# Loading the sample's q and k into the mLSTM's tile ring, and giving a discarded square its own tile, in a hybrid encoder layer

## The chip, the cores and the metric

The kernel runs on one core of a Trainium2 chip. The metric is the device time of one execution in microseconds (us), lower is better. The time of a kernel is the median of several executions.

## The reference, cut to what matters

One layer is applied to two sequences, a prompt of 1024 tokens and a sample of 256 tokens, both of width 2048 in float32:

```
hn   = rmsnorm(x);  proj = hn @ w_in            # 2048 -> 9232 columns
att  = neighbourhood_attention(q, k, v, bias) * silu(g)      # 8 heads of 128, 8 x 16 window on a 64-wide grid
h    = mlstm(forward) + mlstm(backward)         # 4 heads of 256, from conv+silu of proj, v and gates
mem  = rmsnorm_per_head(h) * sigmoid(o) * silu(z)
y    = rmsnorm(x + concat(att, mem) @ w_out)
```

For each head of the attention, softmax(q k^T scale + bias) v is computed over the window of each token. The sample is a grid of 4 rows, so that all 256 of its keys are scored at once. For each mLSTM head, gated scores q k^T, states k^T v and their products with q are formed, the result is normalised by its mean square, and gated.

## The kernel before, in words

Products in float32 are made of three matmuls of "high" and "low" halves of each operand: the `split` helpers (L164 to L169) write the high half with ScalarE and the low half with VectorE. Layouts put the feature or key axis on the 128 partitions.

The work comes in this order. First the projection for tokens 0 to 767 (`first_tiles`, `pair_a`, to about 1050 us), then that for tokens 768 to 1279: `proj_v`, `proj_pair` and `pair_s`. Both write q, k, v, the convolved q and k of the mLSTM and the gates to DRAM (`qS`, `kS`, `vS`, `cS`, `cD`, `pT`). From the point where the pool `ap` is opened, just before `hf` is first used, the rest of the second projection and the attention and mLSTM stage are written down together: `run` (L1303 on) steps two lists of units, one of the mLSTM and one of the attention, under high priority, and the projections left over fill the gaps between them. Last comes the output product (L1613), whose tiles take the memory of `ap` when the stage is over.

The order of each engine's instructions is not written by hand. The tile framework plans it when the kernel is built, with a simulated timeline (`schedule_with_timeline_sim=True`), by priority and by when tiles come free, and each engine then takes its instructions strictly in that order, waiting where something is not there yet. A tile with a tag takes one of `bufs` slots of that tag and frees it after its last reader. All loads of this stage are issued by SyncE (`DM`), one queue in order.

The units that matter here:

- The attention's list has, for each head, `na_sample(h)` and then `na_prompt(h)`. `na_sample` loads q and k of the 256 sample tokens (L799, two DMAs of 256 KB), then v, makes two blocks of scores `nas_0s`, `nas_1s` (L773, in `na_softmax`), transposes and multiplies by v. `na_prompt` loads q and k of the 1024 prompt tokens (L844, L845, two DMAs of 1 MB), then four blocks follow, each with two score products `nap_0s`, `nap_1s` (L773), a softmax, transposes (L790) and the product with v (L886 to L901). One step starts a new unit and moves the older ones on, so the sample's load, the prompt's load together with the sample's scores, and the prompt's first scores are three steps in a row.
- Both q/k tiles carry the tag `nqk` with one buffer: the sample uses a corner of the prompt's 16 KB-per-partition tile.
- The mLSTM's list has, for each head, a unit for the sample, four state units and four output units. Its k, q and v tiles (`load_s`, L1072, and `load_v`, L1085), the weighted keys and the split states (`c_split`) all take slots of one tag `hf`, 8 slots of 4 x 272 floats per partition. `load_c` (L1066) loads keys for transposes `tb` (L1120).
- Decay weights, products and gate tiles of the mLSTM take slots of the tag `sml`, 6 slots. So does `jk` (L1258), into which ScalarE writes a square of which only the row sum is used (L1259); 40 of them are made.

The stage's projections that fill gaps are `pc` (L662) and `pv` (L740), with weight tiles `wr`, `wr_v` (L633) and their halves `ws`, `wsv`.

Of the kernel before, what the change touches and what calls it, by code (L numbers as in the profile page):

```python
# [8 lines left out]
F32 = mybir.dt.float32  # L9
F32R = mybir.dt.float32r  # L10
# [3 lines left out]
P = 128  # L14
D = 2048
KT = D // P
TS = 256
TP = 1024
# [27 lines left out]
def kernel(  # L46
# [23 lines left out]
    def f(ap):  # L70
        return ap.bitcast(F32)

    def bank(tag, name):
        return ps.tile([P, 512], F32, tag=tag, name=name, bufs=3 if tag == "pr" else 5)
# [683 lines left out]
    def hf(name):  # L758
        return ap.tile([P, 4 * VP], F32R, tag="hf", name=name, bufs=8)
# [2 lines left out]
        return ap.tile([P, 512], dt, tag="mid", name=name, bufs=6)[:, :n]  # L762

    def sml(name, n=256, dt=F32):
        return ap.tile([P, 260], dt, tag="sml", name=name, bufs=6)[:, :n]

    def na_tile(tag, shape, name, bufs, dt=F32):
        return ap.tile(shape, dt, tag=tag, name=name, bufs=bufs)

    def na_softmax(nm, qs, ks, nkeys, h, boff):  # L770
        b = bank("a", f"{nm}s")
        for i, (a_, b_) in enumerate(((0, 0), (0, 1), (1, 0))):
            PE.matmul(b[:, :nkeys], qs(a_), ks(b_), start=i == 0, stop=i == 2)  # L773
        bt = na_tile("nbt", [P, NAK], f"{nm}bt", 2)[:, :nkeys]
        DM.dma_start(bt, rpb_tab[h, :, boff : boff + nkeys])
        st = na_tile("nst", [P, NAK], f"{nm}st", 3)[:, :nkeys]
        sm = na_tile("sm", [P, 4], f"{nm}sm", 4)
        V.tensor_tensor_reduce(  # L778
            st, b[:, :nkeys], bt, -1.0, 3.0e38, ALU.add, ALU.min, sm[:, 0:1],
        )  # L780
        S.activation(st, st, AF.Exp, bias=sm[:, 0:1], scale=-1.0, accum_out=sm[:, 2:3])
        V.reciprocal(sm[:, 3:4], sm[:, 2:3])
        S.mul(st, st, sm[:, 3:4])
        return st

    def na_transpose(nm, st, order, dst):
        b = bank("a", f"{nm}t")
        n = len(order)
        for i, c in enumerate(order):
            PE.transpose(b[:, i * P : (i + 1) * P], st[:, c * P : (c + 1) * P], ident)  # L790
        bv = b[:, : n * P].rearrange("p (k q) -> p k q", q=P)
        S.copy(dst[0], bv)
        V.tensor_tensor(dst[1], bv, f(dst[0]), op=ALU.subtract)

    def na_sample(h):
        nm = f"nas{h}"
        qk = na_tile("nqk", [P, 4, TP], f"{nm}qk", 1, F32R)[:, :, :TS]
        for i, src in enumerate((qS[h], kS[h])):
            DM.dma_start(f(qk[:, 2 * i : 2 * i + 2]), src[:, :, TP:])  # L799
        yield  # L800
        v = na_tile("nv", [P, 4, 2, P], f"{nm}v", NV, F32R)
        DM.dma_start(
            f(v[:, :2].rearrange("p t z d -> p t (z d)")),
            vS[h // 2][TP:, (h % 2) * 256 : (h % 2 + 1) * 256].rearrange("(t p) x -> p t x", p=P),
        )
        st = [
            na_softmax(
                f"{nm}_{t}", lambda a_: qk[:, a_, t * P : (t + 1) * P],
                lambda b_: qk[:, 2 + b_, :], TS, h, BIAS_S + t * TS,
            )  # L810
            for t in range(2)
        ]
        yield
        pt = na_tile("npt", [P, 2, 768], f"{nm}pt", 1, F32R)
        for t in range(2):
            na_transpose(
                f"{nm}_{t}", st[t], (0, 1),
                [
                    pt[:, z, :512].rearrange("p (s q) -> p s q", s=2)[:, :, t * P : (t + 1) * P]
                    for z in range(2)  # L820
                ],
            )
        yield
        b = bank("a", f"{nm}o")
        for c in range(2):
            for i, (a_, b_) in enumerate(((0, 0), (0, 1), (1, 0))):
                PE.matmul(
                    b[:, :TS], v[:, c, a_], pt[:, b_, c * TS : (c + 1) * TS],
                    start=c == 0 and i == 0, stop=c == 1 and i == 2,
                )  # L830
        o = na_tile("nst", [P, NAK], f"{nm}ot", 3)[:, :TS]
        DM.dma_start(o, pT[GT0 + h][:, TP:])
        V.scalar_tensor_tensor(o, b[:, :TS], 0.5, o, op0=ALU.mult, op1=ALU.mult)
        DM.dma_start(mixT[h][:, TP:], o)
        yield
# [220 lines left out]
    def ml_units(sq, h, gates):  # L1056
        T, off = (TS, TP) if sq == "s" else (TP, 0)
        nc_ = T // 256
        nm = f"ml{sq}{h}"
# [95 lines left out]
        def out_unit(J):  # L1155
            n2 = f"{nm}_{J}"
# [14 lines left out]
            for st in range(2):  # L1171
                i = 2 * J + st
                sb = bank("a", f"{n2}s{st}")
                for dt in range(2):
                    mm3(
                        sb[:, :256], lambda a_: kk[:, a_, dt, st * P : (st + 1) * P],
                        lambda b_: qt[:, b_, dt, :], dt == 0, dt == 1,
                    )
                for d in range(2):
                    hc = d * 4 + h  # L1180
                    lo_, hi_ = (0, 256) if st == d else (st * P, (st + 1) * P)
                    n = hi_ - lo_
                    dd = sml(f"{n2}d{st}{d}", n)
                    ds = slice(st * P, (st + 1) * P)
                    S.activation(
                        dd[:, st * P - lo_ : st * P - lo_ + P], dm[:, d, ds], AF.Exp,
                        bias=bd[:, i, hc : hc + 1],
                    )
                    if st == d:
                        os_ = slice((1 - st) * P, (2 - st) * P)  # L1190
                        S.activation(
                            dd[:, os_], al[:, d, os_], AF.Exp, bias=bo[:, i, hc : hc + 1]
                        )
                    V.tensor_tensor(dd, dd, sb[:, lo_:hi_], op=ALU.mult)
                    ph = (mid if st == d else sml)(f"{n2}p{st}{d}", 2 * n, F32R)
                    ph = ph.rearrange("p (h c) -> p h c", h=2)
                    split(ph[:, 0], ph[:, 1], dd)
                    for e in range(lo_ // P, hi_ // P):
                        pp[d, e, st] = ph[:, :, e * P - lo_ : (e + 1) * P - lo_]
# [40 lines left out]
            for e in range(2):  # L1240
                for d in range(2):
                    hc = d * 4 + h
                    c = e * 2 + d
                    V.tensor_scalar(
                        r[:, c : c + 1], acc[d, e][:, 256:257], em[:, 2 * J + e, hc : hc + 1], None,
                        op0=ALU.max,
                    )
                    V.scalar_tensor_tensor(
                        r[:, c : c + 1], acc[d, e][:, 256:257], -1.0, r[:, c : c + 1],
                        op0=ALU.mult, op1=ALU.max,  # L1250
                    )
                    V.reciprocal(r[:, c : c + 1], r[:, c : c + 1])
                S.mul(hs[:, e, :], acc[0, e][:, :256], r[:, e * 2 : e * 2 + 1])
                V.scalar_tensor_tensor(
                    hs[:, e, :], acc[1, e][:, :256], r[:, e * 2 + 1 : e * 2 + 2], hs[:, e, :],
                    op0=ALU.mult, op1=ALU.add,
                )
                jk = sml(f"{n2}jk{e}")  # L1258
                S.activation(jk, hs[:, e, :], AF.Square, accum_out=r[:, 4 + e : 5 + e])  # L1259
            rsqrt_mean(r[:, 6:8], r[:, 4:6], 2, 256.0)  # L1260
            yield
# [30 lines left out]
        for J in range(nc_):  # L1292
            yield out_unit(J)
# [161 lines left out]
    ap = att_ctx.enter_context(tc.tile_pool(name="att", bufs=2))  # L1455
# [7 lines left out]
    def paced(units, n):  # L1463
# [3 lines left out]
        return [at.get(j, iter(())) for j in range(n)]  # L1467

    na = [[u for h in (2 * i, 2 * i + 1) for u in (na_sample(h), *na_prompt(h))] for i in range(ML_H)]
    run(  # L1470
        [
# [308 lines left out]
```

## Time and profile before

| | us |
|---|---|
| median of 3 runs | 2563.29 |
| lowest, highest | 2563.03, 2566.54 |
| the profiled execution | 2565.18 |
| its span, first to last instruction | 2563.3 |

The profile is of one execution. Times in it are microseconds from the first instruction. PE is TensorE's matmuls, PEld its weight loads, DVE VectorE, ACT ScalarE, POOL GpSimd, SP SyncE; "SPq" marks instructions that issue a DMA. L773 is line 773 of the kernel. A group is written "line engine operation output<-inputs shape xcount"; a wait is written "who line <- whom: us in total, times, longest us"; a timeline row is "start us, us, engine line operation", with the idle time before it and its releaser in brackets. A chain row is "start us, us, what". Names of tiles leave out buffer numbers, so `nap3qk` is the q/k tile of prompt head 3, `nas3qk` that of sample head 3, `mlp_1k` the k tile of the prompt's output unit 1 of any mLSTM head, and `mls_0k` that of the sample's unit. The granted clock is TensorE's, 1.00 at full speed. A busy TensorE is not TensorE at full clock: a matmul at half clock is busy for longer.

### The profile page before, as it was taken

What the parts mean: (1) busy time and instruction counts of PE and PEld (TensorE: products, weight loads), DVE (VectorE), ACT (ScalarE), POOL (GpSimd) and SP (SyncE); (2) the same over time, 40 slices, a digit from 0 to 9 for tenths busy, and PEclk for the clock granted to TensorE, in tenths of its full rate; (3) what the DMA queues carried; (4) which work ended last, traced back from release to release, by engine and by line L of the source; (5) the groups of instructions that cost most, each with busy time, mean ns of one, the idle gap of its engine ahead of it and who ended that gap; (6) DMA issues with size and microseconds to landing.
All of it is one profiled execution on the core that took longest, in us unless ns stands there. A gap on an engine that the chain in (4) does not pass through costs nothing.

```text
span 2563.3 us, 44540 instructions
## 1 busy us (share of the span) xinstructions
PE 2534.0 (99%) x15054; PEld 2368.6 (92%) x15054; DVE 1972.6 (77%) x4029; ACT 1345.0 (52%) x3041; POOL 615.3 (24%) x909
## 2 busy tenths in 40 slices
PE   8999999999999999999999999999999999999998
PEld 8999999999999999999999999998988887788886
DVE  8769888888869798898875866765855665879695
ACT  8535545444444444465655666655745543344444
POOL 0535555444544444410001110100100104000001
PEclk9999999999999999999999999999999999999999
DMA  6546464536434342467768878877867849636237
GB/s 215 174 143 200 143 199 130 179 124 200 125 112 126 101 141 89 154 228 223 239 223 299 297 243 272 293 234 261 286 197 251 277 126 377 202 125 218 85 87 254
DMA packets 303483, 503.03 MB, mean 196 GB/s; under 512 B 48752, under 2 KB 191256, under 8 KB 303256
## 3 DMA queue, kind: packets, MB, share of 16 engines
q1 hardware_dynamic: 299096, 484.46, 58.9%
q0 software_dynamic: 4160, 15.73, 1.6%
q8 instruction: 119, 1.95, 0.3%
q14 instruction: 108, 0.88, 0.1%
HBM read 373.13 MB, written 126.95 MB: 195 GB/s over the span
## 4 chain that ended last, share of the span: by engine, by line
PE 92%; DMA 5%; DVE 2%; issue 1%; ACT 1%; SPq 0%; POOL 0%; ACTq 0%; POOLq 0%; DVEq 0%
PE pc L662 16%; PE po L1613 14%; PE pv L740 5%; PE fb L274 2%; PE A24b L274 1%; PE A12b L274 1%; PE A16b L274 1%; PE A44b L274 1%; PE A48b L274 1%; PE A52b L274 1%; PE A40b L274 1%; PE A20b L274 1%; PE A8b L274 1%; PE A50b L274 1%; PE A42b L274 1%; PE A22b L274 1%
## 5 line engine op out<-in xcount | busy, mean ns | idle before, releaser
L1613 PE MATMUL po<-wo,mo 128*128 128x512 f32 x1620 | 376.9, 393 | 3.7 <-ACT wo L165 2.8
L1613 PEld LDWEIGHTS po<-wo,mo 128*128 128x128 f32 x1620 | 303.6, 188 | 76.2 <-ACT wo L165 4.2
L166 DVE TENSOR_TENSOR ws<-wr,ws 128x512 fp32r<-128x512 f32 x152 | 104.3, 696 | 53.2 <-ACT ws L165 52.4
L165 ACT CAST ws<-wr 128x512 fp32r<-128x512 f32 x152 | 92.5, 617 | 70.1 <-PE pc L662 57.5
L165 ACT CAST mo<-mb 128x640 fp32r<-128x640 f32 x72 | 51.8, 726 | 92.5 <-PE po L1613 73.7
L116 POOL TENSOR_SCALAR rs<-rs 128x1 f32<-128x1 f32 x10 | 3.4, 341 | 351.2 <-DVE rs L1593 351.1
L166 DVE TENSOR_TENSOR mo<-mb,mo 128x640 fp32r<-128x640 f32 x72 | 59.1, 827 | 27.1 <-ACT mo L165 27.0
L1562 DVE TENSOR_TENSOR y<-y,po 128x512 f32<-128x512 f32 x90 | 58.5, 687 | 11.3 <-PE po L1613 11.0
L165 ACT CAST mo<-ms 128x640 fp32r<-128x640 f32 x40 | 28.9, 726 | 61.1 <-PE po L1613 32.1
L166 DVE TENSOR_TENSOR wsv<-wr_v,wsv 128x512 fp32r<-128x512 f32 x64 | 44.4, 700 | 14.2 <-ACT wsv L165 13.9
L165 ACT CAST wsv<-wr_v 128x512 fp32r<-128x512 f32 x64 | 39.0, 617 | 26.8 <-PE pv L740 15.5
L1576 ACT ACTIVATE jk<-y 128x512 f32<-128x512 f32 x40 | 25.2, 631 | 36.5 <-DVE y L1562 36.2
L413 DVE SCALAR_TENSOR_TENSOR pcv<-pco,cw_sb,pcv 128x516 f32<-128x516 f32 x48 | 36.7, 764 | 7.1 <-ACT pcv L407 7.0
L166 DVE TENSOR_TENSOR mo<-ms,mo 128x640 fp32r<-128x640 f32 x40 | 32.8, 823 | 7.6 <-ACT mo L165 7.6
L129 ACT ACTIVATE xq<-xq 128x1024 f32<-128x1024 f32 x20 | 21.2, 1061 | 31.7 <-DMA xq<-in_xtok_dram 29.2
L1081 POOL MEMSET mls_0v<- 128x2 f32 x4 | 0.4, 102 | 145.1 <-DVE S_dt.float L166 119.7
L274 PE MATMUL fb<-xg,fw 128*128 128x384 f32 x192 | 34.6, 334 | 0.0
L251 DVE TENSOR_TENSOR pco<-pc,rstdb 128x512 f32<-128x512 f32 x30 | 20.6, 687 | 17.8 <-PE pc L662 17.1
L274 PEld LDWEIGHTS fb<-xg,fw 128*128 128x128 f32 x192 | 33.4, 188 | 0.0
L778 DVE CUSTOM_DVE_ANT_0 nap_0st<-nap_0s,nap_0bt 128x384 f32<-128x384 f32 x32 | 17.7, 555 | 20.1 <-PE nap_0s L773 8.7
L1525 DVE TENSOR_TENSOR ms<-mb,mb 128x640 f32<-128x640 f32 x40 | 32.8, 823 | 0.0
L1492 POOL DMA_DIRECT2D mb<-mx x32 | 17.7, 554 | 58.8 <-DVE ws L166 24.8
(2655 smaller groups left out, 8512.4 us busy)
## 6 DMA issues: line engine op xcount, KB each, us to landing
wr<-in_w_in_dram SPq DMA_DIRECT2D x76, 512.0 KB, 4.7
wr_v<-in_w_in_dram SPq DMA_DIRECT2D x32, 512.0 KB, 5.0
wb<-in_w_o_dram SPq DMA_DIRECT2D x48, 256.0 KB, 3.0
xq<-in_xtok_dram SPq DMA_DIRECT2D x20, 512.0 KB, 4.2
mb<-mx POOLq DMA_DIRECT2D x32, 320.0 KB, 8.2
wr_wp<-in_w_o_dram SPq DMA_DIRECT2D x16, 512.0 KB, 4.0
vS<-vo SPq DMA_DIRECT2D x24, 256.0 KB, 5.1
nap_0bt<-in_rpb_tab_dram SPq DMA_DIRECT2D x32, 192.0 KB, 4.3
```

Of the source, the lines that this page charges most:

```text
L129: S.activation(raw, raw, AF.Square, accum_out=ssq[g][:, t, q : q + 1])
L165: S.copy(hi, src)
L166: V.tensor_tensor(lo, src, f(hi), op=ALU.subtract)
L251: V.tensor_tensor(o, src, rb, op=ALU.mult)
L274: PE.matmul(o, w(a_), x(b_), start=first and m == 0, stop=last and m == 2)
L413: V.scalar_tensor_tensor(dst[:, a:n], src[:, a + j - pad : n + j - pad], cw_sb[:, ct, j : j + 1], dst[:, a:n], op0=ALU.mult, op1=ALU.add,)
L662: PE.matmul(pb[j], t[j][:, wi, c : c + P], xs[xi], start=first and m == 0, stop=last and m == 2,)
L740: PE.matmul(outs[tt], xs[:, tt * P : (tt + 1) * P], t[:, wi, q * w : (q + 1) * w], start=first and m == 0 and (gates or tt % 2 == 0), stop ...
L1525: V.tensor_tensor(t, x, y_, op=op)
L1562: V.tensor_tensor(Y[p, q, tt], Y[p, q, tt], bk, op=op)
L1576: S.activation(jk, Y[p, q, tt], AF.Square, accum_out=ss[t][:, c : c + 1])
L1613: PE.matmul(bk[tt], m[xi][:, tt * P : (tt + 1) * P], w[wi], start=first and kk == 0 and j == 0, stop=last and j == 2, skip_group_check=True,)
```

## The change

The q and k of a sample head go into a tile of the `hf` ring (4 x 256 of its 4 x 272 floats) and no longer into the tile that the prompt uses. The discarded square has a tag and a tile of its own with one buffer, and the `sml` tag has 7 slots. Nothing that is computed changes, and no instruction is added or removed.

```diff
     def sml(name, n=256, dt=F32):
-        return ap.tile([P, 260], dt, tag="sml", name=name, bufs=6)[:, :n]
+        return ap.tile([P, 260], dt, tag="sml", name=name, bufs=7)[:, :n]
...
     def na_sample(h):
         nm = f"nas{h}"
-        qk = na_tile("nqk", [P, 4, TP], f"{nm}qk", 1, F32R)[:, :, :TS]
+        qk = hf(f"{nm}qk")[:, : 4 * TS].rearrange("p (i c) -> p i c", i=4)
         for i, src in enumerate((qS[h], kS[h])):
             DM.dma_start(f(qk[:, 2 * i : 2 * i + 2]), src[:, :, TP:])
...
-                jk = sml(f"{n2}jk{e}")
+                jk = ap.tile([P, 256], F32, tag="jk", name=f"{n2}jk{e}", bufs=1)
                 S.activation(jk, hs[:, e, :], AF.Square, accum_out=r[:, 4 + e : 5 + e])
```

## The prediction

> **What bounds the kernel now.** I read the page first, then TensorE's waits, then the stretch of the trace in which the edited lines run.
>
> ```profile
> span 2563.3 us, 44540 instructions
> PE 2534.0 (99%) x15054; PEld 2368.6 (92%) x15054; DVE 1972.6 (77%) x4029; ACT 1345.0 (52%) x3041; POOL 615.3 (24%) x909
> PE 92%; DMA 5%; DVE 2%; issue 1%; ACT 1%; SPq 0%; POOL 0%; ACTq 0%; POOLq 0%; DVEq 0%
> ```
>
> TensorE is busy for 2534.0 of 2563.3 us and carries 92% of the chain that ended last. The change neither adds nor removes a matmul, so directly it can win only idle time of TensorE and time in which TensorE's clock is low. The edited lines run in the attention and mLSTM stage, about 1350 to 2110 us. Its row in the table by windows (TensorE busy first, then weight loads, VectorE, ScalarE, GpSimd, then clock, DMA share, GB/s), and TensorE's waits in the same stretch:
>
> ```profile
> 1350.00:2110.00 760.00, 754.89 (x4813) 684.68 (x4812) 512.76 (x1396) 448.57 (x1114) 68.59 (x252) 1.00 0.78 255
> ```
> ```profile
> PE nap_0s L773 <- DMA nap3qk<-kS: 2.5, 1, 2.5
> PE nap_0s L773 <- DMA nap4qk<-kS: 1.9, 1, 1.9
> PE nap_0s L773 <- DMA nap2qk<-kS: 0.5, 1, 0.5
> ```
>
> TensorE idles 760 - 754.89 = 5.11 us here, and three waits make up 2.5 + 1.9 + 0.5 = 4.9 us of it: the first prompt scores of heads 3, 4 and 2 wait for the prompt's k. All else in the stage, ScalarE at 448.57 and VectorE at 512.76 of 760 us among it, lies beside a full TensorE.
>
> Why that k is late can be read at head 3, from SyncE's queue, TensorE's timeline and the chain (start, duration, what):
>
> ```profile
> 1594.95 0.68 PE L773 MATMUL nap_1s<-nap2qk 128*128 128x384 f32 x3
> ...
> 1595.66 0.53 SPq L799 DMA_DIRECT2D nas3qk<-qS  x1
> ```
> ```profile
> 1619.46 0.51 PE L773 MATMUL nas_1s<-nas3qk 128*128 128x256 f32 x3
> ```
> ```profile
> 1623.45 0.52 SPq L844 DMA_DIRECT2D nap3qk<-qS  x1
> 1624.02 0.60 SPq L845 DMA_DIRECT2D nap3qk<-kS  x1
> ```
> ```profile
> 1624.02 10.22 DMA nap3qk<-kS
> 1634.25 0.14 issue
> 1634.38 0.76 PE nap_0s L773 x3
> ```
>
> One buffer serves in turn: prompt 2's last scores (1594.95), then sample 3's load (1595.66), then sample 3's last scores (1619.46), and only then the prompt's two loads of 1 MB (1623.45, 1624.02). The second takes 10.22 us, and TensorE, in its written order, stands before it for 2.54 us.
>
> **What a stall costs beside itself.** TensorE's clock in windows of 2 us, at the 0.5 us stall of head 2, after that of head 3 and after that of head 4 (the clock is the third number from the end):
>
> ```profile
> 1554.00:1556.00 2.00, 1.50 (x10) 1.47 (x10) 0.38 (x2) 0.00 (x0) 0.00 (x0) 1.00 1.10 343
> 1634.00:1636.00 2.00, 1.62 (x10) 1.61 (x11) 0.82 (x3) 0.00 (x0) 0.00 (x0) 0.92 1.08 361
> 1636.00:1638.00 2.00, 2.00 (x11) 2.00 (x11) 1.83 (x6) 1.93 (x6) 1.04 (x3) 0.50 1.10 386
> 1638.00:1640.00 2.00, 2.00 (x15) 2.00 (x15) 1.35 (x5) 0.20 (x2) 0.73 (x4) 0.73 1.01 405
> 1734.00:1736.00 2.00, 2.00 (x9) 2.00 (x10) 0.97 (x3) 0.00 (x0) 0.60 (x1) 0.66 1.02 412
> 1736.00:1738.00 2.00, 2.00 (x11) 2.00 (x10) 1.55 (x7) 1.17 (x4) 0.00 (x0) 0.50 1.02 348
> 1738.00:1740.00 2.00, 2.00 (x18) 2.00 (x18) 0.81 (x3) 1.68 (x6) 0.00 (x0) 0.98 0.87 230
> ```
>
> After the 2.5 us stall the clock falls short by (0.08 + 0.50 + 0.27) x 2 us = 1.7 us of full speed; after the 1.9 us stall by (0.34 + 0.50 + 0.02) x 2 = 1.7 us. After 0.5 us nothing. TensorE counts as busy meanwhile, so this 3.4 us stands in no idle column.
>
> [...]
>
> **The change part by part.**
>
> Prompt's buffer. With the sample elsewhere, the loads of L844 and L845 wait only for the previous prompt's last scores: at head 3 they could be issued at about 1595.7 instead of 1623.45, 27.7 us sooner. Landing in 10.2 us, as in this row, they are there by about 1606, before the sample's scores at 1619.46 and 28 us ahead of their own. Heads 2 and 4 are built alike. If TensorE's first prompt scores keep their place behind the sample's, all three stalls go: -4.9 us, and with the two long ones -3.4 us of low clock. Bounds: nothing (the planner pulls the scores up to the earlier landing) and -8.3 us. I take -8.3: the sample's scores, too, stand 24 us behind the issue of their load, which needs 5 (below), so the stream is held there by something other than loads, and the prompt's first scores come after it.
>
> Sample's load. The same two DMAs of 256 KB go into one of eight "hf" tiles; no instruction is added. Their time to landing, from the tile of sample 1:
>
> ```profile
> DMA to landing us min/median/max: 4.5/4.7/5.0
> ```
>
> The new wait is on SyncE, for a free slot; behind it stand bias tiles, weights and the mLSTM's own loads. Such waits exist already:
>
> ```profile
> SPq L1085 <- PE mlp_0s L1095: 10.7, 3, 5.0
> ...
> SPq L799 <- PE pc L662: 7.7, 2, 7.2
> ```
>
> The new one is bounded by the longest ring wait, 5.0 us; the old one on L799, up to 7.2 us, goes. What the borrowed slot delays is a prefetch, and those have room:
>
> ```profile
> 1428.01 0.52 SPq L1072 DMA_DIRECT2D mlp_1k<-cS  x1
> ```
> ```profile
> 1461.37 0.52 PE L1095 MATMUL mlp_1s<-mlp_1q,mlp_1k 128*128 128x256 f32 x3
> ```
> ```profile
> 1516.43 1.33 SPq L1085 DMA_DIRECT2D mlp1a2v<-vS  x1
> ```
> ```profile
> 1564.00 0.77 PE L1095 MATMUL mlp1a2kv<-mlp1a2v,mlp1a2w 128*128 128x258 f32 x5
> ```
>
> One is used 33 us after issue, the other 48; a slot held from load to scores (24 us at head 3) fits. I take 0. Without that room each late tile of 512 KB would cost up to the 5.0 us of a ring wait.
>
> The jk tile and seven "sml" slots. Nothing but ScalarE writes jk, nothing reads it:
>
> ```profile
> L1259 ACT ACTIVATE mlp_2jk<-mlp_2hs x8: 417/418/420, 1516.1 to 2074.6; 128x256 f32<-128x256 f32 x8
> ```
>
> Forty squares stay forty at 0.42 us on an engine with 311 us free in the stage. Two requests fewer per mLSTM unit and one slot more can only loosen that chain; TensorE idles 5.11 - 4.9 = 0.2 us for everything else there, so the gain is 0 to 0.2 us. I take 0. A loss could come only through the rearranged order of the stage, which is the third rival.
>
> End of the stage. It has room too:
>
> ```profile
> 2113.31 0.34 PE L901 MATMUL nap_3o<-nap_3pt,nap_3v 128*128 128x128 f32 x2
> ```
> ```profile
> 2185.08 12.99 PE L1613 MATMUL po<-wo,mo 128*128 128x512 f32 x55 [0.47 <-DVE wo L166]
> 2199.01 1.65 PE L1613 MATMUL po<-wo,mo 128*128 128x512 f32 x6 [0.94 <-ACT wo L165]
> ```
>
> The last attention matmul is at 2113.31, and gate projections fill some 70 us until the output product at about 2183. An earlier or later end of attention by 10 us is absorbed. The small idles here, 0.47 + 0.94 = 1.4 us, may come or go.
>
> **Sum.** The profiled execution took 2565.18 us: 2565.2 - 4.9 - 3.4 = **2556.9**, I say 2557. That execution is 1.9 us above the median, 2563.29 us (2563.03 to 2566.54), so against the median it is -6.3 us, -0.25%. About 0.2%, 5.1 us, is what a measurement of this kernel can tell from no change: faster is below 2558.2, slower above 2568.4.
>
> **Rivals.**
>
> 1. The sample's load becomes the late one, because a slot comes free late. It lands in 4.5 to 5.0 us, half the prompt's time; half of 4.9 us in pieces too short for a dip is 2.5 us: 2556.9 + 2.5 = 2559.4, the same. For it: SyncE's ring waits. Against: its room of 24 - 5 = 19 us at head 3. 0.13.
>
> 2. It does not do what it says: the first scores are pulled up to the landing, the stalls only move in time, 2563 to 2565, the same. For it: TensorE's place at head 3 (1634.38 - 2.54 = 1631.8) is 7.8 us behind the load's issue, about a load's time, so the planner may set it by the load. 0.07.
>
> 3. Slower: the moved 2 MB crowd out loads that have no room. At the start of the stage (the window's clock, DMA share and GB/s last; then the chain):
>
> ```profile
> 1370.00:1380.00 10.00, 9.88 (x78) 9.42 (x77) 4.33 (x16) 5.11 (x12) 0.13 (x2) 1.00 1.04 404
> ```
> ```profile
> 1363.74 7.47 DMA mlp0a3cv<-cD
> 1371.22 0.04 issue
> 1371.26 0.33 PE mlp0a3tb L1120
> ```
> ```profile
> 1370.94 0.52 SPq L844 DMA_DIRECT2D nap0qk<-qS  x1
> ```
>
> The DMA engines are full, the tile for the transposes at 1371.26 lands as it is needed, and prompt 0's loads, now behind it, need no longer wait for the sample's scores. Put ahead of it they delay it by 2 MB / 404 GB/s = 5.2 us, and with a dip of 1.7 us TensorE loses 6.9 us. One such place takes back most of the gain (2563.8); from two on it decides (2570.7); three give 2556.9 + 20.7 = 2577.6. Eight head changes offer the chance. For it: the whole order of the stage is replanned, and TensorE takes its queue in order, whatever is late. Against: room of 33 and 48 us above. 0.30.
>
> 4. The dips come from something other than the stalls and stay: only 4.9 us go, 2565.2 - 4.9 = 2560.3, the same. That both stand right behind the two long stalls speaks against it. 0.05. [...]
>
> My forecast keeps 0.45; its own range is 2553 (the 1.4 and 0.2 us of small idles go too, and the 1.9 us by which the profiled execution is above the median) to 2560.5 (the stall of 1.9 with its dip of 1.7 stays), and 0.40 of it lies below 2558.2. So faster 0.40; same 0.05 + 0.13 + 0.07 + 0.05 = 0.30; slower 0.30. For 8 in 10 the range goes from 2553 to 2578, past three crowded loads, leaving some 0.05 below and 0.12 above.
>
> **What would show it.** Right: no wait of the first prompt scores on their q and k, the prompt's loads issued within a few us of the previous prompt's last scores, TensorE idle under 1 us between 1350 and 2110, no window there with a clock near 0.5. Wrong: waits of TensorE on the sample's tile (rival 1), on the same tile still (2), on mLSTM, v or weight tiles behind a prompt's load (3). A long idle at the output product's start would show that the end of attention had no room after all.

## The result and the profile after

The changed kernel takes 2573.20 us (median of 6 runs, 2572.02 to 2575.65), the kernel before, run beside it, 2562.86 us (6 runs, 2559.49 to 2566.54). The ratio is 1.0043, with a 95% interval of 1.0032 to 1.0055: 10.3 us slower. In a second comparison (e5 below) it is 1.0048 (1.0036 to 1.0060).

The page of the changed kernel, profiled in an execution of 2575.65 us (span, then engines):

```profile
span 2573.9 us, 44495 instructions
...
PE 2536.9 (99%) x15054; PEld 2367.3 (92%) x15054; DVE 1968.2 (76%) x4029; ACT 1338.6 (52%) x3041; POOL 611.5 (24%) x909
```

TensorE is busy for 2.9 us longer than before (2536.9 against 2534.0 us). The shares of the chain that ended last can't be set against those of before: TensorE's reads 75% here, 88% in a second profile of the changed kernel and 37% in a second one of the kernel before, and what is missing up to 100% is the first part of the span, over which the chain was not followed. The table by windows, for the stage and for the 90 us behind it, in which the last gate projections end and the output product begins (TensorE busy first; clock third from the end), of after and then of before:

```profile
1350.00:2110.00 760.00, 752.75 (x4834) 681.77 (x4834) 507.40 (x1399) 445.48 (x1116) 66.54 (x252) 1.00 0.80 255
2110.00:2200.00 90.00, 83.47 (x347) 66.47 (x346) 46.26 (x70) 25.08 (x42) 28.73 (x52) 0.96 0.93 341
```
```profile
2110.00:2200.00 90.00, 86.63 (x374) 69.23 (x374) 52.50 (x79) 27.23 (x44) 28.65 (x52) 1.00 0.90 337
```

Idle time in the stage went up, from 5.11 to 7.25 us, and behind it from 3.37 to 6.53 us, with a clock of 0.96. TensorE's waits show that they are other waits:

```profile
PE po L1613 <- ACT wo L165: 3.8, 1, 3.8
PE mlp_0tp L1266 <- DVE mlp_0hs L1264: 2.0, 1, 2.0
PE pc L662 <- ACT ws L165: 2.0, 2, 1.4
PE pc L662 <- DVE ws L166: 1.6, 2, 1.3
...
```

No wait of the first prompt scores (nap_0s) on their q and k is left. At head 3 it can be seen why; SyncE's queue, then TensorE, of the changed kernel:

```profile
1601.69 0.53 SPq L844 DMA_DIRECT2D nap3qk<-qS  x1
1602.28 0.60 SPq L845 DMA_DIRECT2D nap3qk<-kS  x1
1604.25 0.53 SPq L799 DMA_DIRECT2D nas3qk<-qS  x1
```
```profile
1600.98 0.68 PE L773 MATMUL nap_1s<-nap2qk 128*128 128x384 f32 x3
...
1623.98 0.52 PE L773 MATMUL nas_0s<-nas3qk 128*128 128x256 f32 x3
...
1635.52 0.69 PE L773 MATMUL nap_0s<-nap3qk 128*128 128x384 f32 x3
```

The prompt's loads go out 0.03 us after the previous prompt's last scores end (1601.66), 22 us sooner than before, and now ahead of the sample's. They are used 33 us later. So the change does what it says, and pays elsewhere. Two such places, in rows of the changed kernel: in the middle of the stage (SyncE, ScalarE, TensorE), where a load of 2 KB comes late for ScalarE's first convolution tap, and TensorE's queue, in its written order, stands behind what ScalarE and VectorE have yet to do; and at the output product's start. The chain rows put below those of the first stall show why the small load is late.

```profile
1471.38 0.42 SPq L671 DMA_DIRECT2D pco<-qb  x1
```
```profile
1476.56 0.82 ACT L407 ACTIVATE pcv<-pco,cb_sb,cw_sb 128x516 f32<-128x516 f32 x1 [2.85 <-DMA pco<-qb]
```
```profile
1478.49 0.44 PE L1266 MATMUL mlp_0tp<-ident,mlp_0hs 128*128 128x128 f32 x2 [1.96 <-DVE mlp_0hs L1264]
```
```profile
1464.12 6.82 DMA mx<-nap0o
...
1471.00 0.33 SPq L847
...
1471.38 5.08 DMA pco<-qb
```
```profile
2109.42 0.33 PE L901 MATMUL nap_3o<-nap_3pt,nap_3v 128*128 128x128 f32 x2
...
2178.69 11.57 PE L1613 MATMUL po<-wo,mo 128*128 128x512 f32 x38 [3.82 <-ACT wo L165]
```
```profile
2178.00:2180.00 2.00, 1.31 (x3) 1.12 (x4) 1.33 (x3) 1.98 (x4) 0.00 (x0) 0.50 1.04 396
2180.00:2182.00 2.00, 2.00 (x6) 1.52 (x6) 1.17 (x2) 0.20 (x1) 0.00 (x0) 0.50 1.04 391
2182.00:2184.00 2.00, 2.00 (x7) 1.52 (x6) 0.00 (x0) 0.00 (x0) 0.00 (x0) 0.50 1.06 401
```

At 1478 us SyncE stands until the store of prompt 0's output has freed the tile for the gate of prompt 1 (L847), and the 2 KB behind it go out 5.2 us ahead of their use. Prompt 1's q and k are not what they stand behind: these were issued some 44 us earlier and landed within 10.1 us. At the end, the last attention matmul comes 3.9 us earlier than in the first profile of before (2109.42 against 2113.31), and yet the output product waits 3.82 us for its weights, with three windows at 0.50 behind the wait.

**One account for all kernels.** For each profile I added up, over windows of 2 us from 1350 to 2260 us, TensorE's idle time and the part of its busy time that a clock under 1.00 lost. It is this sum by parts, in us (the names of the experiments are explained below):

| kernel | 1350 to 1400 | to 1700 | to 2100 | to 2260 | sum | span |
|---|---|---|---|---|---|---|
| before, first profile | 0.1 | 4.8 | 3.6 | 3.8 | 12.3 | 2563.3 |
| before, second, third | 0.0, 0.0 | 3.2, 5.1 | 0.0, 0.2 | 3.6, 3.6 | 6.8, 8.9 | 2558.3, 2560.8 |
| changed, first profile | 1.6 | 5.0 | 0.8 | 9.3 | 16.7 | 2573.9 |
| changed, second (e5) | 1.9 | 5.3 | 0.8 | 8.4 | 16.4 | 2570.4 |
| e1 sample's tile alone | 1.6 | 6.9 | 4.0 | 4.9 | 17.5 | 2568.6 |
| e2 square and slot alone | 0.0 | 1.8 | 0.1 | 2.0 | 4.0 | 2555.7 |
| e4 own tile | 1.8 | 2.4 | 1.2 | 8.3 | 13.7 | 2566.0 |
| e3 k stays | 0.5 | 0.5 | 0.0 | 2.1 | 3.1 | 2554.4 |
| e6 head 0 held | 0.0 | 3.0 | 3.5 | 9.4 | 15.9 | 2567.4 |
| e7 columns ahead | 1.6 | 0.0 | 0.0 | 8.9 | 10.5 | 2568.5 |
| e8 burst written later | 3.7 | 5.9 | 0.6 | 9.9 | 20.1 | 2573.0 |
| e9 burst held | 1.7 | 5.2 | 0.9 | 5.1 | 12.9 | 2568.6 |
| e10 all three | 0.0 | 2.4 | 2.6 | 1.9 | 6.9 | 2560.1 |
| e12 slot alone | 0.0 | 0.8 | 0.2 | 2.6 | 3.5 | 2556.1 |
| e15 before, burst held | 0.0 | 4.3 | 0.0 | 0.8 | 5.1 | 2557.0 |
| e16 e2, burst held | 0.1 | 1.0 | 0.9 | 0.8 | 2.7 | 2557.6 |
| e17 columns by GpSimd | 2.2 | 1.2 | 0.7 | 9.8 | 13.9 | 2567.2 |
| e18 small loads by GpSimd | 7.2 | 0.2 | 0.2 | 4.1 | 11.7 | 2568.6 |
| e11 fastest | 0.0 | 0.0 | 0.0 | 0.9 | 0.9 | 2549.7 |

Span less sum is 2549 to 2555 us in all but four rows (changed first, e7, e9, e18), whose profiled executions came to the stage some 4 to 6 us late, with TensorE's instructions ahead of the stage the same. So the kernels differ mainly by idle and low clock in this stretch. The changed kernel's 16.5 against a mean of 9.3 in the three profiles of before are 7 of the 10 us: 5.2 of them at the end, 1.7 at the start, and 0.8 up to 1700 us, where one set of stalls takes the place of another, less 0.5 up to 2100 us. 1 more is idle time in the output product from 2200 to 2500 us (1.4 and 1.8 us against 0.4, 0.0 and 0.7), and the last 2 I did not place.

### The profile page after: what moved, and what is told of

The parts are those of the page before. It is cut to its first block, busy times and chain, and to the rows that moved or that the text cites. A ratio compares the mean times of both kernels' runs of the same rounds, so it can differ in the third digit from the quotient of the medians.

```text
span 2573.9 us, 44495 instructions
## 1 busy us (share of the span) xinstructions
PE 2536.9 (99%) x15054; PEld 2367.3 (92%) x15054; DVE 1968.2 (76%) x4029; ACT 1338.6 (52%) x3041; POOL 611.5 (24%) x909
## 3 DMA queue, kind: packets, MB, share of 16 engines
q8 instruction: 119, 1.95, 0.3%
## 4 chain that ended last, share of the span: by engine, by line
PE 75%; DMA 5%; DVE 5%; issue 1%; ACT 1%; SPq 0%; POOL 0%; ACTq 0%; POOLq 0%; DVEq 0%
PE pc L662 15%; PE po L1613 10%; PE pv L740 4%; PE A16b L274 1%; PE A44b L274 1%; PE A40b L274 1%; PE A48b L274 1%; PE A52b L274 1%; PE A20b L274 1%; PE A54b L274 1%; PE A46b L274 1%; PE A22b L274 1%; PE A18b L274 1%; PE A70b L274 1%; PE A38b L274 1%; PE A50b L274 1%
## 5 line engine op out<-in xcount | busy, mean ns | idle before, releaser
L165 ACT CAST wsv<-wr_v 128x512 fp32r<-128x512 f32 x64 | 39.0, 617 | 26.9 <-PE pv L740 12.9
L274 PE MATMUL fb<-xb,fw 128*128 128x384 f32 x96 | 23.9, 356 | 7.8 <-ACT fw L172 7.8
```

The costliest lines, as they stand in the source:

```text
L165: S.copy(hi, src)
L274: PE.matmul(o, w(a_), x(b_), start=first and m == 0, stop=last and m == 2)
```

## The experiments

Theories: **A**, the prompt's 2 MB, issued earlier (22 us at head 3), come in the way of loads that are asked for just ahead of their use; **B**, the borrowed slot makes the sample's load or the ring late; **C**, the part with the square; **D**, any edit makes the planner write another order with other late places; later **E**, for the end.

**e1, the sample's tile alone; e2, the square's tile and the seventh slot alone.**

```diff
# e1: before, and
+        qk = hf(f"{nm}qk")[:, : 4 * TS].rearrange("p (i c) -> p i c", i=4)
# e2: the changed kernel, but
+        qk = na_tile("nqk", [P, 4, TP], f"{nm}qk", 1, F32R)[:, :, :TS]
```

> Only the sample's q and k move to the hf ring; the square stays in a sml tile and sml keeps 6 slots. Four theories of the loss of 10.3 us. A (moved prompt loads: the 2 MB that now start 12 to 28 us earlier make small and just-in-time loads late, those of the 4 boundary columns qb above all): near the changed kernel, 2573 us, with the same stalls behind the convolution's first tap. B (borrowed slot: the sample's load waits for a free hf slot and is late): near 2573 too. C (the square's tile and the seventh sml slot rearranged the stage): the forecast's 2557. D (every edit makes the planner write a new order with late places of its own, whichever edit it is): another time anywhere from 2557 to 2578, with stalls at other places.

> Only the square gets a tile of its own and sml a seventh slot; sample and prompt share one q/k buffer as before. A and B: 2563, with the three waits of the first prompt scores as before. C: 2573. D: another time between 2557 and 2578, although the sml ring was no bottleneck.

e1: 2568.95 us against 2560.18, ratio 1.003 (1.002 to 1.004), with waits behind ScalarE and the gate rows (`zr`) in the middle of the stage, so at other places than in the changed kernel. e2: 2557.53, ratio 0.9989 (0.9980 to 0.9998), and no wait of the first prompt scores is left although the buffer is still shared: there the prompt's k lands in at most 9.5 us (10.2 us at head 3 before), and TensorE's order has the scores 10 us behind its issue. C falls; the sample's move carries the loss. The waits went because the order moved, which is D at work.

**e3, the sample's k in the shared buffer, its q in the ring; e4, both in a tile of their own.**

```diff
# e3, in place of the two loads (the scores then read k from kk)
+        kk = na_tile("nqk", [P, 4, TP], f"{nm}k", 1, F32R)[:, 2:4, :TS]
+        DM.dma_start(f(qk[:, 0:2]), qS[h][:, :, TP:])
+        DM.dma_start(f(kk), kS[h][:, :, TP:])
# e4
+        qk = na_tile("nsq", [P, 4, TS], f"{nm}qk", 1, F32R)
-        return ap.tile([P, 4 * VP], F32R, tag="hf", name=name, bufs=8)
+        return ap.tile([P, 4 * VP], F32R, tag="hf", name=name, bufs=7)
```

> The changed kernel, but the sample's k stays in the buffer shared with the prompt and only its q takes an hf slot: the prompt's loads are held back until the sample's scores, as before, while the ring still lends a slot. A: back to 2563 (the crowding goes, the stalls of 8.3 us return). B: 2573 or more. D: neither follows; stalls at other places than in both kernels.

> The changed kernel with the sample's q and k in a tile of their own (4 KB per partition), and the hf ring cut from 8 slots to 7 to make room. The prompt's loads are free to go early as in the changed kernel, the sample's load waits for no ring slot. A: 2573 or more. B as a late sample's load: 2563 or less, with the sample's loads back at their earlier places; B as a shortage of ring slots: above 2573, since the ring has 7 all the time. D: another time.

e3, which lends the slot but holds the prompt's loads: 2555.64, ratio 0.9983 (0.9974 to 0.9992), better than A had said, since nearly no stall came back. e4, which lends nothing but lets the prompt's loads go: 2567.39, ratio 1.003 (1.0018 to 1.0041), with the same long idle at the output product and, in addition, waits of 1.3 and 1.1 us for the sample's q. B as the main cause falls; freeing the prompt's loads is what the slow kernels have in common: the changed kernel, e1 and e4 are 3.0 to 4.8 parts in 1000 slower than before, while e2, e3 and e12 (below), which hold them, are 0.4 to 1.7 parts faster (e12 no more than no change can be). Each has an order of its own, so D alone would hardly part them like this, though it settles where each of them loses.

**e5, the changed kernel again.**

> The changed kernel once more, for a second profile. Its first profile is 4.2 us longer than that of before already at the end of the second projection (1351.64 against 1347.46 us), where TensorE's instructions are the same; if that belongs to the one execution, it is gone here (1347 to 1348, as in the four runs so far) and the time is 2569 to 2573; if it belongs to the kernel, 1351 again. The start of the transposes stays 27 to 27.5 us behind the end of the second projection by theory A (23.8 before).

2573.96, ratio 1.0048. The end of the second projection is at 1348.21: the 4.2 us ahead of the stage were that one execution's. The rest came back as in the first profile (16.4 against 16.7 us).

**e6, head 0 held.**

```diff
+        if h:
+            qk = hf(f"{nm}qk")[:, : 4 * TS].rearrange("p (i c) -> p i c", i=4)
+        else:
+            qk = na_tile("nqk", [P, 4, TP], f"{nm}qk", 1, F32R)[:, :, :TS]
```

> The changed kernel, but sample 0 alone keeps its q and k in the buffer shared with the prompt, so that prompt 0's loads are held as before; the other seven heads are free. Theory A: the start of the transposes is back at 23.5 to 24.3 us behind the end of the second projection, 3.3 us sooner than in the changed kernel, and the time falls by about 3.3 us if the rest of the stage stays. Theory B (borrowed slots): no gain at the start. Theory D: the rest of the stage is replanned too, so that the total can go either way by 5 us while the start obeys A.

2566.48, ratio 1.0022 (1.0013 to 1.0030), 7.5 us less than the changed kernel beside it (the profiled execution, 2569.14 us, gained less). The transposes start 23.7 us behind the end of the second projection (27.0 in e5), and the idle there is gone, 1.9 to 0.0 us. VectorE's first bias table shows the crowd, in e6 and then in the first profile of the changed kernel:

```profile
1366.95 0.42 DVE L778 CUSTOM_DVE_ANT_0 nas_0st<-nas_0s,nas_0bt 128x256 f32<-128x256 f32 x1 [1.06 <-DMA nas_0bt<-in_rpb_tab_dram]
```
```profile
1376.20 0.42 DVE L778 CUSTOM_DVE_ANT_0 nas_0st<-nas_0s,nas_0bt 128x256 f32<-128x256 f32 x1 [5.51 <-DMA nas_0bt<-in_rpb_tab_dram]
```

TensorE does not stand before the late tile itself: its order has the transposes later, behind all the `pv` matmuls, and what is then bare is the time of the splits between transposes and their product. The idle near 1458 us went too, with a new order; the end stayed.

**e7, the boundary columns loaded ahead.**

```diff
...
+    for ct in range(16):
+        if QK0 + ct // 2 * 2 not in SECOND:
+            DM.dma_start(qbt[:, ct], qb[ct])
...
-                DM.dma_start(o[:, 0:4], qb[ct])
+                G.tensor_copy(o[:, 0:4], qbt[:, ct])
```

> The changed kernel, but the 4 boundary columns of each convolution of the late projections are loaded ahead of the stage into one small tile, and GpSimd copies them in place of a load of 2 KB by SyncE at each use. By theory A with its detail (the small loads queue behind the 1 MB ones, ScalarE waits 2.7 to 3.4 us for them at its first tap, and TensorE's queue after it), the stalls at 1461, 1478 and 1650 us (1.4 + 2.0 + 1.4 us) go: 4.8 us less. If the small loads are bystanders, ScalarE's waits go but the stalls of TensorE stay.

2570.25, ratio 1.0035 (1.0023 to 1.0047), 3.7 us less. TensorE's busy time from 1400 to 1700 us, in e7 and in e5:

```profile
1400.00:1700.00 300.00, 299.96 (x2023) 277.04 (x2022) 219.29 (x604) 191.86 (x482) 33.84 (x115) 1.00 0.84 273
```
```profile
1400.00:1700.00 300.00, 296.18 (x1996) 273.60 (x1996) 216.84 (x605) 188.25 (x475) 30.04 (x103) 0.99 0.84 270
```

The stalls behind the small loads are gone, all of them. The gain in time is less certain, since the two intervals overlap.

**e8 and e9, the burst at the end.**

```diff
# e8: the 16 tiles of Ac and Aa are written down inside the product
+        if p == 0 and i == 2:
+            Ac.append(mix_block(1, 1, kk))
+        if p == 0 and i == 5:
+            Aa.append(mix_block(0, 0, kk))
# e9: at the same places, behind the step's split, with a tie to its operand
+        V.tensor_copy(t[:, 0:1], f(after[:, 0:1]))
+        G.dma_start(t, mixT[8 * kh + kk][:, th * TH : (th + 1) * TH])
```

> The changed kernel, but of the 10.5 MB that GpSimd loads for the output product in one burst from about 2115 us on, the half that the second and third product need first is asked for only when these products are written down. Theory E (the end of attention came 4 us sooner, the burst with it, and it starves the weight loads of the late gates and of the output product): the wait of 3.8 us at 2179 us, the two of 1.3 to 1.4 us before it and the clock dip behind it go, 6 to 9 us less. If the burst is a bystander: no change in TensorE's waits from 2110 to 2190 us.

> The changed kernel with the burst really held: each of the 16 loads of the second half (5.2 MB) goes into a tile of which VectorE first writes one column, out of the split operand of the second product's first or second step, so that GpSimd cannot load it before. Sixteen copies of one column are added. Theory E (the burst that follows the end of attention starves the last gate weights and the output product's first weights): TensorE's waits on these weights between 2110 and 2190 us (2.2 + 1.3 + 4.4 us in the second profile of the changed kernel) and the clock dip fall to the 1 to 3 us of the kernel before, 6 to 9 us less, 2565 to 2568. If the burst is a bystander (the gate projections are simply further behind): no change, or slower, since the held loads can be late for the second product.

e8: 2574.67, ratio 1.0048. It tells nothing: 31 of these loads are still issued between 2110 and 2190 us, since the planner moved them up as soon as their memory was free. e9: 2566.60, ratio 1.0021 (1.0012 to 1.0031), 6.6 and 7.4 us below the changed kernel's two medians (5.6 and 6.9 us by the ratios, 3 to 4 us in the account above). TensorE's waits from 2110 us on, in the changed kernel and in e9:

```profile
PE po L1613 <- ACT wo L165: 3.8, 1, 3.8
PE pc L662 <- ACT ws L165: 1.4, 1, 1.4
PE pc L662 <- DVE ws L166: 1.3, 1, 1.3
```
```profile
PE pc L662 <- DVE ws L166: 1.9, 1, 1.9
PE pc L662 <- ACT ws L165: 1.5, 1, 1.5
```

The wait at the output product goes, the two in the gate projections stay, beside the first half of the burst, which is not held. But that the burst starved the product is not shown by it. What the product waits for is one weight load (`wr_wp`, 512 KB). Its issue by SyncE and the product's first matmuls, in the kernel before, the changed kernel and e9, then its landing in the changed kernel:

```profile
2153.86 1.47 SPq L633 DMA_DIRECT2D wr_wp<-in_w_o_dram  x1
```
```profile
2160.00 7.10 PE L1613 MATMUL po<-wo,mo 128*128 128x512 f32 x30
```
```profile
2163.31 1.11 SPq L633 DMA_DIRECT2D wr_wp<-in_w_o_dram  x1
```
```profile
2167.75 7.12 PE L1613 MATMUL po<-wo,mo 128*128 128x512 f32 x30
```
```profile
2160.33 0.33 SPq L633 DMA_DIRECT2D wr_wp<-in_w_o_dram  x1
```
```profile
2169.86 15.46 PE L1619 MATMUL po<-wo,mo 128*128 128x512 f32 x66
```
```profile
2163.31 14.63 DMA wr_wp<-in_w_o_dram
```

It takes 14.6 us to land in the changed kernel and still 13.4 us in e9 (the median of the 16 loads of its kind is 4.8 us in the changed kernel). But it is issued 4.4 us ahead of the product's first matmul in the changed kernel, 6.1 us in the kernel before, and 9.5 us in e9, whose order is another. Over all profiles the wait goes with that lead: 3.8 to 5.2 us of wait where the lead is 3.4 to 4.4 us (changed twice, e4, e6, e7, e8, e17), 1.3 to 1.8 us where it is 6.1 to 6.6 us (before three times, e2, e3, e18), and none in the product's first 20 us where it is 8.6 us or more (e1, e9 to e12, e16). An earlier burst, as E has it, does not go with it: its first load is at 2113.17 and 2114.95 us in the two later profiles of the kernel before (e13, e14), and at 2115.13 and 2111.73 us in those of the changed kernel. So by these rows the load's place in SyncE's order makes most of this wait. That is read from the profiles; no run changed the place alone.

**e10, all three at once; e11, e3 with the burst held; e12, the seventh slot alone.**

> The changed kernel with all three suspects taken away at once: head 0's sample back in the shared buffer, the boundary columns loaded ahead, the burst held. Seven heads keep their early prompt loads. If the loss of 10 to 12 us is these three places (3.3 at the start, 3 to 5 at the small loads, 4 to 6 at the end), the stage takes 805 to 808 us from the end of the second projection to the output product (816 in the changed kernel, 812.5 before), and the time is 2557 to 2561, less some us that the 8 small loads cost ahead of the stage. If early loads cost something everywhere else too: 2565 or more.

> The fastest kernel so far (the sample's k in the shared buffer, its q in the ring, own tile for the square, seven slots) with the burst held. By theory E, 0 to 3 us less than 2555.6, since its waits at the output product's start are only 2.6 us. If holding delays the second product: slower.

> The kernel before with nothing but the seventh sml slot; the square stays in the ring. It splits the gain of the square's part (2.6 us by medians, and the three waits on the prompt's k gone although the buffer is still shared). If the extra slot is the cause: 2557 to 2558. If the square's own tile is: 2560 to 2561 with the three waits. By theory D (the planner's order moves with any edit): neither, 2555 to 2570.

e10: 2561.05, ratio 0.9998 (0.9990 to 1.0007): with the three places gone nearly all of the loss is gone, and seven heads of early loads remain. Set against the kernel before with the burst held (e15 below, 0.9989), a loss of 2 us may be left; the intervals overlap. The early loads bring nothing: 2.4 and 2.6 us of new idle stand behind other small loads (`mlp_0zr`, `nas5ot`), and the way from the end of the second projection to the output product takes 812.2 us, not the 805 to 808 expected. e11: 2552.89, ratio 0.9966 (0.9953 to 0.9978), the fastest of all. Its window of the stage:

```profile
1350.00:2110.00 760.00, 760.00 (x4856) 688.65 (x4855) 517.55 (x1404) 451.20 (x1119) 73.40 (x260) 1.00 0.79 258
```

TensorE is never idle in the stage. e12: 2559.91, ratio 0.9996 (0.9987 to 1.0005): the extra slot cannot be told from no change, nor from e2. The waits for the prompt's k are gone here too, with one slot more and nothing else, which is D again.

**e13 and e14, before again.**

> The kernel before once more, for a second profile. Its first profile (2565.18 us) lies at the top of the runs of before (medians 2560.2 to 2562.9), and the forecast took its three waits for the prompt's k (4.9 us) and two clock dips (3.4 us) for every execution's. If they belong to the kernel: the same three waits and dips, 812 to 813 us from the end of the second projection to the output product. If they belong to that execution (a load that lands 2 us later than others): less of them, 804 to 809 us, and about 2557 to 2562 in all.

> The kernel before a third time, for the spread of the same waits. As for the second: the waits for the prompt's k of heads 2, 3 and 4 either again 4.9 us with both dips, or another number.

2560.17 and 2562.65 us. The waits for the prompt's k, in e13 and in e14:

```profile
PE nap_0s L773 <- DMA nap3qk<-kS: 1.6, 1, 1.6
...
PE nap_0s L773 <- DMA nap2qk<-kS: 0.5, 1, 0.5
```
```profile
PE nap_0s L773 <- DMA nap3qk<-kS: 1.8, 1, 1.8
...
PE nap_0s L773 <- DMA nap2qk<-kS: 0.6, 1, 0.6
```

2.1 and 2.4 us, not 4.9; head 4's 1.9 us does not come back, and one dip is left in e14, none in e13. From the end of the second projection to the output product it is 807.5 and 809.5 us, so the first profile's 812.5 were that execution's.

**e15, before with the burst held; e16, e2 with the burst held.**

> The kernel before with the burst held as in the two runs that held it, nothing else changed. It tells whether the end's gain needs the change at all. By theory E, 2 to 4 us less than before (the changed kernel gained 7.4, the fastest one 2.8): 2557.5 to 2559.5. If the gain came from undoing what the change did: 0.

> Own tile for the square and seven slots, both q and k of the sample in the shared buffer, and the burst held. It tells whether moving the sample's q alone is worth anything beside the other two: by the difference of the two kernels without the hold (2557.5 against 2555.6), 2554 to 2556 here against 2552.9; if the q's move is worth nothing, 2553.

e15: 2558.73, ratio 0.9989 (0.9980 to 0.9998); e16: 2558.25, ratio 0.9982 (0.9974 to 0.9991). Holding the burst gains by itself: in e15 the weight load has a lead of 6.6 us, close to the 6.1 us of before, and yet no wait at the product's start is left, and the stretch from 2100 us on costs 0.8 us instead of 3.6 to 3.8. So the burst does count, by some 3 us, in the kernel before as well. e16 is above the 2554 to 2556 us expected. Moving the sample's q alone, e11 over e16, is worth 1.6 parts in 1000, but the intervals touch, so that stays open.

**e17, the boundary columns issued by GpSimd; e18, all small loads.**

```diff
# e17
+                G.dma_start(o[:, 0:4], qb[ct])
# e18: also
+        G.dma_start(bt, rpb_tab[h, :, boff : boff + nkeys])
+                    G.dma_start(o_, pT[OT0 + ch][:, c0 : c0 + na])
+                    G.dma_start(zn, pT[ZT0 + ch][:, c0 : c0 + na])
+        G.dma_start(o, pT[GT0 + h][:, TP:])
```

> The changed kernel, but the loads of 2 KB of boundary columns (12 of them) are issued by GpSimd instead of SyncE, at the same point of the program. Are they late because of their place in SyncE's one queue, or because the DMA engines are full? Place in the queue: ScalarE's waits for them at 1457, 1473 and 1642 us and the stalls of TensorE behind them go, as in the kernel that loads them ahead (2570.3), 2569 to 2571. Full engines: they land as late as before, 2573 to 2574. A new order of the stage can cover either by some us, so the waits for these loads decide, not the time alone.

> As the one before, and also the bias tables (128 to 192 KB), the mLSTM's gate rows and the sample's gate (up to 128 KB) are issued by GpSimd, so that SyncE's queue holds the large loads, the weights and the stores. If the loss of the changed kernel is small loads behind large ones in one queue: the idle at the stage's start (1.6 to 1.9 us) and between 1400 and 1700 us (3.8 to 5 us) goes, about 5 us less, 2567 to 2569, while the end (8.4 to 9.3 us of idle and low clock) stays. If GpSimd, which waits up to 46 us for mLSTM tiles, holds them up instead: slower than 2574.

e17: 2568.69, ratio 1.0021 (1.0013 to 1.0030). ScalarE's waits at the first tap in the stage and, of the line that loads the columns, the time to landing: e5, then e17.

```profile
ACT pcv L407 <- DMA pco<-qb: 18.0, 5, 5.3
```
```profile
DMA to landing us min/median/max: 2.8/5.0/6.4
```
```profile
ACT pcv L407 <- DVE wsv L166: 1.5, 1, 1.5
```
```profile
DMA to landing us min/median/max: 1.9/5.1/6.4
```

They take as long to land, but nobody waits for them any more: they are asked for further ahead. Of the 12 loads 8 are used less than 6 us after their issue in the changed kernel's first profile, 6 in e5 and 5 in the kernel before, 2 in e17. (ScalarE waits 9.6 us for them in the first profile of the changed kernel, 5.7 us in the kernel before.) So their place in SyncE's order made them late, with a landing of 5 us in either case. One such load does stand behind a prompt's k, as A has it. In e5 SyncE, before it issues the load that ScalarE then waits 5.28 us for at 1437.65 us, stands until prompt 1's k has landed:

```profile
SPq L671 <- DMA nap1qk<-kS: 3.5, 1, 3.5
```

But TensorE is not idle there. Where it is, at 1461, 1478 and 1650 us in the first profile, the last prompt's loads had been issued 33 us or more before. Issued by another engine these loads land no faster, 5.1 us in e17 against 5.0 us in e5 (the medians); what helped is the time at which they are issued.

e18: 2566.85, ratio 1.0015 (1.0006 to 1.0024). From 1400 to 2100 us 0.4 us is left, and the end is at 4.1 us, half of what was expected to stay. At the start the third rival's place shows (SyncE, then TensorE):

```profile
1363.31 0.52 SPq L845 DMA_DIRECT2D nap0qk<-kS  x1
1375.32 0.95 SPq L1066 DMA_DIRECT2D mlp0a3cv<-cD  x1
```
```profile
1382.84 1.24 PE L1120 MATMUL mlp0a3tb<-ident,mlp0a3cv 128*128 128x128 f32 x4 [3.78 <-DMA mlp0a3cv<-cD]
```

The tile for the transposes is issued 12 us behind prompt 0's k, and costs 3.78 us of wait and, by the account above, 2.8 us of clock: 6.6 us. Prompt 0's 2 MB are only a part of what it stands behind: SyncE issues two of prompt 0's v loads (L858) in between, which alone take 6.0 us of its time.

## Why the prediction was wrong

It forecast 2557.0 us, faster by 6.3 us; the kernel is slower by 10.3 us, and inside the range only because the range reached over the third rival.

- **The prompt's buffer: mechanism right, size wrong.** The loads go out as forecast and the waits go. But the 8.3 us were one execution's: by the two more profiles of before the waits and dips are 2.1 us (e13) and 4.0 us (2.4 + 1.6, e14).
- **Room, read as "What the borrowed slot delays is a prefetch, and those have room": a step that failed.** The slot was harmless (e3 lends it and is faster than before). What failed is that room was read from two large prefetches, with 33 and 48 us between issue and use, and that everything the moved 2 MB and a new order could make late was put at nothing from it. Other loads have no room: 8 of the 12 loads of boundary columns are used 2.7 to 5.9 us after their issue and take 4.7 us to land (the median). The cost is 1.6 to 1.9 us at the start of the stage, where holding head 0's loads takes it away (e6), and 5.0 to 5.3 us up to 1700 us, which mostly takes the place of the 3.2 to 5.1 us lost there before. That the prompt's loads themselves delay the small ones is seen at the start (the bias table) and at 1437 us; at the stalls of TensorE in the middle it is the order of SyncE's queue, and how the freed loads led to that order stays open.
- **The end, "absorbed": failed too, and is the largest single loss.** The stretch from 2100 us on costs 9.3 and 8.4 us, 3.6 to 3.8 before. The row at 2185.08 us was read as the output product's start, with 70 us of gate projections ahead of it; the product's first matmul is at 2160.00 us, 47 us behind attention's last (58 us in the changed kernel). It waits for a weight load that was issued 4.4 us ahead of it and took 14.6 us. The prediction named the sign that would show it ("A long idle at the output product's start") and put no price on it. Why the new order issues that load so late is open: e1 and e18, with early loads and no hold, issue it 8.6 and 6.6 us ahead and have a better end (4.9 and 4.1 us).
- **The square and the seventh slot, taken at 0:** 0.9989 (0.9980 to 0.9998) for the two and 0.9996 for the slot; right within what a measurement can tell.
- **The dips** do follow stalls, as taken: the clock goes down to 0.50 behind each of the five stalls of 2.35 us or more that are listed in the last section. The fourth rival falls.
- **The third rival** had the outcome and one of its places, the start of the stage, where the changed kernel loses 1.6 to 1.9 us and not 6.9. That its sum for two such places, 2570.7, lies near the result is luck: most of the loss stands at the end. So is e18's price (6.6 us against 6.9), of 3.8 us of wait and 2.8 of clock where the rival had 5.2 and 1.7. It was wrong on which loads are hurt, and in hindsight its chance of 0.30 was low.

## What to carry to other kernels

When a load is set free to start earlier, look at the loads used soonest after their issue, the smallest too, and set the time between their issue and use against the time that they take to land: here 2.7 to 5.9 us against 4.7 us, and 4.4 us against 14.6 us at the end. Room of 33 us at one load says nothing of another in the same queue. A dependence that looks like waste may be what keeps a prefetch out of the way, and a wait seen in one profile should be looked for in a second one before it is counted. Where a stage ends, ask also what the next one loads, and when it asks for it.

## What the runs showed of the hardware

Not every stall of the same length is followed by a dip of the clock. In the first profiles of before and of the changed kernel and in those of e17 and e18, from 1350 to 2260 us, five stalls of TensorE are of 2.35 us or more: 2.54 us (before), 3.82 us (changed), 2.35 and 4.60 us (e17) and 3.78 us (e18). Behind each of them there is a window of 2 us at 0.50. Behind all stalls of up to 1.45 us the clock stays at 1.00. In between it goes either way: 0.50 behind 1.86 us (before, head 4), 1.00 behind 1.83 us (before, at the output product), 1.95 us (e17, at 1377 us) and 1.96 us (changed, at 1478 us). The same wait of 1.81 us at head 3, in e14 with a dip and in e15 with none (the wait, then the window behind it):

```profile
1634.59 0.76 PE L773 MATMUL nap_0s<-nap3qk 128*128 128x384 f32 x3 [1.81 <-DMA nap3qk<-kS]
```
```profile
1636.00:1638.00 2.00, 2.00 (x11) 1.93 (x10) 1.87 (x5) 1.21 (x4) 0.85 (x3) 0.50 1.10 381
```
```profile
1635.55 0.76 PE L773 MATMUL nap_0s<-nap3qk 128*128 128x384 f32 x3 [1.81 <-DMA nap3qk<-kS]
```
```profile
1636.00:1638.00 2.00, 2.00 (x17) 1.97 (x16) 1.66 (x6) 0.91 (x3) 0.00 (x0) 1.00 1.06 329
```

The 1.81 us thus cost no more than themselves in e15, and 1.6 us of clock besides in e14, 1.0 us of it in the row at 0.50 above; behind the 1.86 us of before it was 1.7 us. From these numbers I estimate that the dip alone spreads the times of one kernel by up to 1.7 us a place.
